# Rotary products and the probabilities' lower halves from GpSimd to VectorE in a two-layer attention and retention trunk

## The chip, the cores and the metric

The kernel runs on one core of a Trainium2 chip. Its engines are TensorE (PE in the profile; PEld is its loading of stationary operands), VectorE (DVE), ScalarE (ACT), GpSimd (POOL) and SyncE (SP), which here issues nearly all DMA transfers. The metric is the device time of one execution in microseconds. The time given for a kernel is the median of its runs; in addition one execution is recorded by the hardware profiler, and the profile comes from that one.

## What is computed

Two layers act on 2048 tokens of 1024 elements in float32. In each, the normed input is multiplied by a 1024 x 4096 matrix, whose columns are cut into the query, key, value and gate of eight attention heads of 64 and of four retention heads of 128.

```python
def hybrid_layer(x, norm_gain, w_in, w_out, rel_bias, cos, sin):
    hn = rms_norm(x, norm_gain)
    proj = hn @ w_in
    aq, ak, av, ag, rq, rk, rv, rg = jnp.split(proj, cuts, axis=-1)
    ya = chunked_rel_attention(aq, ak, av, rel_bias)      # 8 heads, own chunk of 64 + 8 before
    yr = chunkwise_retention(rq, rk, rv, cos, sin)        # 4 heads, rotary on rq and rk
    y = jnp.concatenate([ya * silu(ag), yr * silu(rg)], axis=-1)
    return x + y @ w_out

def apply_rotary(t, cos, sin):
    t1, t2 = jnp.split(t, 2, axis=-1)
    return jnp.concatenate([t1 * c - t2 * s, t1 * s + t2 * c], axis=-1)
```

The attention is a softmax over a band of nine chunks with a learned bias by distance. The retention multiplies masked, decayed products of rq and rk with rv, adds rq times a running state, and norms the result. A last rms_norm closes the trunk. The output is float32.

## The kernel before

**Split products.** [...] Every float32 operand is kept as an upper half (the value rounded to float16) and a lower half (what the rounding left), and a product is the sum of three: upper by upper, upper by lower, lower by upper. In the names, `whT`/`wlT` and `whV`/`wlV` are the two halves of the weights, `hTh`/`hTl` those of the normed tokens, transposed. An upper half is usually a copy by ACT; the lower half is a subtraction that follows.

**Loops.** Each of the two layers l has four sections s, each with two attention heads and one retention head. Within a section the tokens run in four blocks n of 512. For each (l, s, n) there are two dense passes. `dense_T` (L608 to 735) makes q, k, rq and rk (j = 0 to 3), each by 24 matmuls of 128 x 512: eight k-tiles times three split products. `dense_V` (L737 to 773) makes values and gates for four tiles a of 128 tokens (v, rv and the two gates, side by side in 512 columns), again 24 matmuls each. So each pass has 96 matmuls, cut by `yield` into 12 rounds of eight. In block (0, 0, 0), marked `first`, `dense_T` has a path of its own, since the weights and tokens are still arriving.

**What runs between the rounds.** `run` (L1117) steps a dense pass. After each round, `tick` fires the steps that were deferred with `later(k, fn)`: fn is issued k rounds later. Then comes one step of the attention generator of the block before, and then some steps of background work, given with `push(generator, steps)` and drawn by `pull` in proportion to the rounds left. The background work prepares the next weights (`prep_T`, `prep_V`, `prep_O`: load, squares, scale, two halves), norms tokens, and in section 2 takes the squares of the output weights (`prep_Omax`, L493: eight loads of 512 KB, a square by ACT for each, L309, and a sum by VectorE), from which the output weights' scale follows.

**Order.** PE, ACT, DVE and POOL run their instructions in program order, so what stands first on an engine's queue holds up what is behind it. SP's order is written out by hand up to the end of the first `dense_V`; after that the scheduler sets it.

**Rotary (L656 to 703).** ACT copies the raw product of rq or rk to `raw` (L662; for rq, `raw` is a view of the tile `rot`). `swap` has SP exchange its two halves of 64 partitions into `swp` with two transfers (L666, L667). Three rounds later (four for the first rq) `turn` issues three operations of 128 x 512 float32 on POOL: raw by the cosine table `tabc` (L670), swp by the sine table `tabs` (L671), and their sum (L672). Then ACT makes the upper half (L675), DVE the lower (L678), ACT a scaled copy for rq (L681), and for rk a transposing transfer makes `kt` (L685). `swp`, `tabc` and `tabs` have one buffer each, and `k`'s halves share the buffer of `swp`.

**Attention (L776 to 852).** There are eight units per block (four tiles of 128 queries by two heads), one in each three rounds. `qk` makes the scores S (L798, L799); DVE adds the bias and takes the maximum (L802, L804); ACT takes the exponential (L805) and copies the upper half into `pq` (L807); POOL subtracts to get the lower half (L808); one round later SP transposes both halves by a transfer into `pT` (L810). Two units later `pv` multiplies them with the values (L818 to 820), and DVE divides and gates (L824 to 830). A unit has 640 keys; in block 0 its four tiles have 128, 256, 384 and 512.

**Retention (L863 to 914).** One of four tiles in each two units. The first products (rk by rq) go in the first round of an even unit; then, by one round each, the mask by DVE (L872), the upper half by ACT (L857), the rest by DVE (L861, tile `dT`). The second products read `dT`, the values and the state's halves `sh` in the third round of the odd unit, five rounds after the first. POOL takes the power for the norm (L906). Both helpers for matmuls stand at L853.

**Bias.** At block 0 of a section, `bias_tiles` loads two bias tiles from a scratch in memory (`toep`), POOL fills two corners (L579, L580), and ACT scales (L581).

## Time and profile before

| | us |
|---|---|
| median of three runs | 2119.16 (2116.42 to 2122.45) |
| the profiled execution | 2117.65 |
| its span, first to last instruction | 2115.9 |
| TensorE busy in the span | 2010.4 |
| mean granted TensorE clock | 0.987 |

How to read the lines below. A row of the groups has line, engine, operation, output and input tile, shapes and count, then the busy time in all, the mean of one in ns, and the idle time of the engine just before these instructions with what ended it. A row of the waits has the engine and line that waited, what it waited for, then total, number and longest. A row of the timeline has start, duration and instruction, and in brackets how long the engine had been idle and what released it. SPq is SP's queue of issues. The profile has 40 equal slices of the span, 52.9 us each; a digit is a tenth of busy time, or of the clock that was granted to TensorE. "issue" is idle time without a recorded cause.

### The profile page before, as it was taken

What the parts mean: (1) busy time and instruction counts of PE and PEld (TensorE: products, weight loads), DVE (VectorE), ACT (ScalarE), POOL (GpSimd) and SP (SyncE); (2) the same over time, 40 slices, a digit from 0 to 9 for tenths busy, and PEclk for the clock granted to TensorE, in tenths of its full rate; (3) what the DMA queues carried; (4) which work ended last, traced back from release to release, by engine and by line L of the source; (5) the groups of instructions that cost most, each with busy time, mean ns of one, the idle gap of its engine ahead of it and who ended that gap; (6) DMA issues with size and microseconds to landing.
All of it is one profiled execution on the core that took longest, in us unless ns stands there. A gap on an engine that the chain in (4) does not pass through costs nothing.

```text
span 2115.9 us, 39456 instructions
## 1 busy us (share of the span) xinstructions
PE 2010.4 (95%) x14014; PEld 1052.1 (50%) x14014; DVE 1253.8 (59%) x3839; ACT 1139.1 (54%) x2522; POOL 679.5 (32%) x701
## 2 busy tenths in 40 slices
PE   6778999999999999988999999999999999999998
PEld 4334555555455555544444555555545555554543
DVE  7677566655565655566653556555656566556643
ACT  7455665556655654555444546554665465446432
POOL 1233333433343433321002343434333433433200
PEclk9899999999999999999999999999999999999999
DMA  8767675558665764699875556555685567548874
GB/s 247 165 119 164 137 164 113 115 110 191 148 113 111 159 158 99 132 197 259 206 187 115 121 103 140 123 124 103 149 186 119 101 137 169 123 101 182 217 193 127
DMA packets 645701, 313.63 MB, mean 148 GB/s; under 512 B 459232, under 2 KB 602080, under 8 KB 645504
## 3 DMA queue, kind: packets, MB, share of 16 engines
q1 hardware_dynamic: 645504, 311.12, 66.5%
q8 instruction: 109, 1.79, 0.4%
q14 instruction: 88, 0.72, 0.1%
HBM read 123.26 MB, written 41.98 MB: 78 GB/s over the span
## 4 chain that ended last, share of the span: by engine, by line
PE 47%; DMA 3%; ACT 2%; DVE 2%; issue 1%; POOL 1%; SPq 1%; POOLq 0%; DVEq 0%; ACTq 0%
PE dT L730 14%; PE dV L750 14%; PE dO L1090 12%; DMA pT<-pq 2%; PE r L853 2%; PE S L799 1%; PE S L798 1%; PE o L818 1%; PE o L819 1%; PE o L820 1%; DVE sc L802 1%; ACT sc L805 0%; ACT pq L807 0%; DMA yhy<-rhy 0%; DMA bias<-toep 0%
## 5 line engine op out<-in xcount | busy, mean ns | idle before, releaser
L808 POOL TENSOR_TENSOR pq<-sc,pq 128x640 f16<-128x640 f32 (+4 forms) x256 | 319.9, 1250 | 930.1 <-ACT pq L807 562.5
L805 ACT ACTIVATE sc<-sc,mq,cT 128x640 f32<-128x640 f32 (+4 forms) x256 | 218.5, 853 | 653.8 <-DVE rl L824 330.4
L730 PE MATMUL dT<-hTh,whT 128*128 128x512 f16 x1008 | 386.0, 383 | 11.9 <-DVE rv L766 7.8
L750 PE MATMUL dV<-wlV,hTh 128*128 128x512 f16 x1024 | 389.1, 380 | 6.9 <-DVE wlV L333 6.9
L750 PE MATMUL dV<-whV,hTh 128*128 128x512 f16 x1024 | 389.3, 380 | 6.2 <-DVE gt L768 6.1
L730 PE MATMUL dT<-hTl,whT 128*128 128x512 f16 x1008 | 386.2, 383 | 4.6 <-DMA hTl<-hTl 2.9
L750 PE MATMUL dV<-whV,hTl 128*128 128x512 f16 x1024 | 389.0, 380 | 0.0
L730 PE MATMUL dT<-hTh,wlT 128*128 128x512 f16 x1008 | 385.7, 383 | 0.0
L730 PEld LDWEIGHTS <-whT 128*128 128x128 f16 x2016 | 195.9, 99 | 236.7 <-issue 20.4
L750 PEld LDWEIGHTS <-hTh 128*128 128x128 f16 x2048 | 197.7, 98 | 223.9 <-DVE gt L768 9.1
L802 DVE CUSTOM_DVE_ANT_0 sc<-S,bias 128x640 f32<-128x640 f32 (+4 forms) x256 | 188.8, 737 | 154.7 <-PE S L799 150.8
L1090 PE MATMUL dO<-whO,yhy 128*128 128x512 f16 x512 | 194.8, 381 | 1.9 <-DMA yhy<-rhy 1.9
L1090 PE MATMUL dO<-whO,yly 128*128 128x512 f16 x512 | 194.6, 380 | 0.8 <-DMA yly<-rly 0.8
L1090 PE MATMUL dO<-wlO,yhy 128*128 128x512 f16 x512 | 194.6, 380 | 0.0
L807 ACT ACTIVATE pq<-sc 128x640 f16<-128x640 f32 (+4 forms) x256 | 171.5, 670 | 11.1 <-DMA pT<-pq 3.0
L1090 PEld LDWEIGHTS <-yhy 128*128 128x128 f16 x1024 | 99.9, 98 | 117.2 <-DMA yhy<-rhy 2.6
L750 PEld LDWEIGHTS <-hTl 128*128 128x128 f16 x1024 | 100.3, 98 | 115.8 <-issue 9.9
L730 PEld LDWEIGHTS <-wlT 128*128 128x128 f16 x1008 | 99.3, 98 | 106.4 <-issue 4.3
L818 PE MATMUL o<-v,pT 128*128 128x65 f16 x1120 | 129.8, 193 | 15.6 <-DMA pT<-pq 15.5
L798 PE MATMUL S<-k,q 128*128 128x128 f16 (+3 forms) x592 | 142.3, 267 | 0.7 <-DVE mq L802 0.7
L818 PEld LDWEIGHTS <-pT 128*128 128x128 f16 x1120 | 105.7, 97 | 51.0 <-DMA pT<-pq 21.5
L819 PE MATMUL o<-v,pT 128*128 128x64 f16 x1120 | 130.0, 195 | 0.0
(350 smaller groups left out, 3499.3 us busy)
## 6 DMA issues: line engine op xcount, KB each, us to landing
q<-qq SPq DMA_DIRECT2D x128, 128.0 KB, 2.5
yyy<-y_d SPq DMA_DIRECT2D x32, 512.0 KB, 4.6
stT<-in_w_in_dram SPq DMA_DIRECT2D x27, 512.0 KB, 4.8
stV<-in_w_in_dram SPq DMA_DIRECT2D x26, 512.0 KB, 4.4
k<-kk SPq DMA_DIRECT2D x128, 64.0 KB, 2.1
swp<-rot SPq DMA_DIRECT2D x64, 128.0 KB, 2.6
tabc<-tab SPq DMA_DIRECT2D x32, 256.0 KB, 2.7
tabs<-tab SPq DMA_DIRECT2D x32, 256.0 KB, 3.1
```

Source lines behind the costliest of these rows:

```text
L730: pe.matmul(ps, w_[:, j, kt, :], h_[:, kt, :], start=(m == 0), stop=(m == 23))
L750: pe.matmul(ps, h_[:, kt, a * P:(a + 1) * P], w_[:, kt, :], start=(m == 0), stop=(m == 23))
L798: pe.matmul(o, st.q[:, hx, 0, cs], k_, start=True, stop=False)
L799: pe.matmul(o, st.q[:, hx, 1, cs], k_, start=False, stop=True)
L802: dve.tensor_tensor_reduce(out=v, in0=S[:, 0:w], in1=g.bias[hx][:, 640 - w:640], scale=1.0, scalar=-3.0e38, op0=ALU.add, op1=ALU.max, accu ...
L805: act.activation(v, v, AF.Exp, bias=m[:, 0:1], scale=g.c[:, 0:1])
L807: act.activation(pq[:, 0:w], v, AF.Copy)
L808: pool.tensor_tensor(pq[:, w:2 * w], v, pq[:, 0:w], op=ALU.subtract)
L818: pe.matmul(o[:, 0:65], u.p[:, b, :], v_[:, 0:65], start=(b == 0), stop=False)
L819: pe.matmul(o[:, 0:64], u.p[:, b, :], v_[:, 65:129], start=False, stop=False)
L853: pe.matmul(out_, w_, m_, start=(i == 0), stop=(i + 1 == len(pairs)))
L1090: pe.matmul(ps, h_[:, kt, :], w_[:, kt, :], start=(m == 0), stop=(m == 23))
```

## The change

There are five edits.

1. The three rotary operations go from POOL to DVE and are issued one per round, in rounds d, d + 1 and d + 2 after the swap, instead of all three in round d. The upper half follows in d + 3, the lower in d + 4, the scaled copy in d + 5 (outside the first block it was d + 6). In the first block rq's d is 5 instead of 4, rk's swap is issued 8 rounds after its copy instead of 5, and its transposition 8 rounds after the swap instead of 7.
2. The lower half of the probabilities goes from POOL to DVE, one round after `qk` instead of in it, and the transposing transfer goes two rounds after `qk` instead of one.
3. `prep_Omax` is pushed in block 2 of section 2 instead of in block 0, again before the value pass.
4. In `dense_T`, tile j = 0 takes its 24 matmuls product by product: first whT by hTh for all eight k-tiles, then wlT by hTh, then whT by hTl. In `dense_V`, tile a = 0 takes all vh by hh, all vh by hl, then all vl by hh. The other tiles go k-tile by k-tile as before, with the three products in the new order.
5. In the retention of block (0, 0, 0) (`slow`) both kinds of products are issued in a unit's third round: the first products two rounds later than before, the second where they were.

```diff
-                    def turn():
-                        pool.tensor_tensor(raw, raw, st.tabc, op=ALU.mult)
-                        pool.tensor_tensor(swp, swp, st.tabs, op=ALU.mult)
-                        pool.tensor_tensor(raw, raw, swp, op=ALU.add)
+                    def turned(out_, x_, y_, op):
+                        return lambda: dve.tensor_tensor(out_, x_, y_, op=op)
...
-                    d = 4 if j == 2 and first else 3
-                    later(d, turn)
-                    later(d + 2 if first else d + 3, upper)
-                    later(d + 3 if first else d + 4, lower)
+                    d = 5 if j == 2 and first else 3
+                    later(d, turned(raw, raw, st.tabc, ALU.mult))
+                    later(d + 1, turned(swp, swp, st.tabs, ALU.mult))
+                    later(d + 2, turned(raw, raw, swp, ALU.add))
+                    later(d + 3, upper)
+                    later(d + 4, lower)
                     if j == 2:
-                        later(d + 4 if first else d + 6, third)
-                    if j == 3:
-                        later(7 if first else 11, tokens)
+                        later(d + 5, third)
+                    else:
+                        later(d + 5 if first else 11, tokens)
...
-                    later(5 if first else 2, swap)
+                    later(8 if first else 2, swap)
...
-            for kt in range(KT):
-                for (w_, h_) in ((g.h, hh), (g.h, hl), (g.l, hh)):
-                    pe.matmul(ps, w_[:, j, kt, :], h_[:, kt, :], start=(m == 0), stop=(m == 23))
+            terms = ((g.h, hh), (g.l, hh), (g.h, hl))
+            order = [(kt, w) for w in terms for kt in range(KT)] if j == 0 else [(kt, w) for kt in range(KT) for w in terms]
+            for kt, (w_, h_) in order:
+                pe.matmul(ps, w_[:, j, kt, :], h_[:, kt, :], start=(m == 0), stop=(m == 23))
...
-            for kt in range(KT):
-                for (w_, h_) in ((g.vh, hh), (g.vl, hh), (g.vh, hl)):
-                    pe.matmul(ps, h_[:, kt, a * P:(a + 1) * P], w_[:, kt, :], start=(m == 0), stop=(m == 23))
+            terms = ((g.vh, hh), (g.vh, hl), (g.vl, hh))
+            for kt, (w_, h_) in ([(kt, w) for w in terms for kt in range(KT)] if a == 0 else
+                                 [(kt, w) for kt in range(KT) for w in terms]):
+                pe.matmul(ps, h_[:, kt, a * P:(a + 1) * P], w_[:, kt, :], start=(m == 0), stop=(m == 23))
...
-            pool.tensor_tensor(pq[:, w:2 * w], v, pq[:, 0:w], op=ALU.subtract)
+            later(1, lambda: dve.tensor_tensor(pq[:, w:2 * w], v, pq[:, 0:w], op=ALU.subtract))
             u.p = b2.tile([P, 10, P], F16, tag="pT", name=f"pT{u.nm}")[:, 0:2 * nb, :]
-            later(1, lambda: sp.dma_start_transpose(out=u.p, in_=pq[:, 0:2 * w]))
+            later(2, lambda: sp.dma_start_transpose(out=u.p, in_=pq[:, 0:2 * w]))
...
+        slow = (l, s, n) == (0, 0, 0)
         for i, (a, hx) in enumerate(units):
             flow(1)
             u = qk(a, hx)
-            if i % 2 == 0:
+            if i % 2 == 0 and not slow:
                 next(ret, None)
             yield
             yield
-            if i % 2 == 1:
+            if i % 2 == 1 or slow:
                 next(ret, None)
...
-                if n == 0 and s == 2:
+                if n == 2 and s == 2:
                     push(prep_Omax(l, go), 13)
```

More of the change, by code (lines that the diff above doesn't have):

```diff
@@ L727, in dense_T @@
             m = 0
-            for kt in range(KT):
-                for (w_, h_) in ((g.h, hh), (g.h, hl), (g.l, hh)):
-                    pe.matmul(ps, w_[:, j, kt, :], h_[:, kt, :], start=(m == 0), stop=(m == 23))
-                    m += 1
-                    if m in (8, 16) or (m == 24 and first):
-                        yield
+            terms = ((g.h, hh), (g.l, hh), (g.h, hl))
+            order = [(kt, w) for w in terms for kt in range(KT)] if j == 0 else [(kt, w) for kt in range(KT) for w in terms]
+            for kt, (w_, h_) in order:
+                pe.matmul(ps, w_[:, j, kt, :], h_[:, kt, :], start=(m == 0), stop=(m == 23))
+                m += 1
+                if m in (8, 16) or (m == 24 and first):
+                    yield
             evacuate(j, ps)
@@ L747, in dense_V @@
             m = 0
-            for kt in range(KT):
-                for (w_, h_) in ((g.vh, hh), (g.vl, hh), (g.vh, hl)):
-                    pe.matmul(ps, h_[:, kt, a * P:(a + 1) * P], w_[:, kt, :], start=(m == 0), stop=(m == 23))
-                    m += 1
-                    if m in (8, 16):
-                        yield
+            terms = ((g.vh, hh), (g.vh, hl), (g.vl, hh))
+            for kt, (w_, h_) in ([(kt, w) for w in terms for kt in range(KT)] if a == 0 else
+                                 [(kt, w) for kt in range(KT) for w in terms]):
+                pe.matmul(ps, h_[:, kt, a * P:(a + 1) * P], w_[:, kt, :], start=(m == 0), stop=(m == 23))
+                m += 1
+                if m in (8, 16):
+                    yield
             rv = gp.tile([P, 3, P], F16, tag="rv", name=f"rv{nm}_{a}")
```

## The prediction

> **What bounds the kernel now.** I read the page first, then the waits of TensorE, the groups by shape, the windows of single stages, and the timeline wherever a wait named its place.
>
> ```profile
> span 2115.9 us, 39456 instructions
> PE 2010.4 (95%) x14014; PEld 1052.1 (50%) x14014; DVE 1253.8 (59%) x3839; ACT 1139.1 (54%) x2522; POOL 679.5 (32%) x701
> PE   6778999999999999988999999999999999999998
> PEclk9899999999999999999999999999999999999999
> ```
>
> TensorE is busy 95% of the span; its poorer slices are the first four (0 to 212 us) and the two where the layers meet. The change takes no matmul away, so all it can win lies in the 105.5 us in which TensorE is not busy and in the stretches at reduced clock. Who owns those 105.5 us is in TensorE's waits (total us, times, longest):
>
> ```profile
> PE r L853 <- DVE dT L861: 15.6, 10, 5.3
> PE o L818 <- DMA pT<-pq: 15.5, 11, 2.3
> PE r L853 <- ACT dT L857: 9.2, 3, 4.5
> PE dT L730 <- DVE rv L766: 7.8, 1, 7.8
> PE dV L750 <- DVE wlV L333: 6.9, 5, 1.6
> PE dV L750 <- DVE gt L768: 6.1, 5, 2.1
> PE dT L730 <- DMA hTl<-hTl: 2.9, 1, 2.9
> ```
>
> So the waits are few and long, not spread over 32 passes; each can be looked up. VectorE (59%) and GpSimd (32%) have room on average, but an average says nothing of a stage.
>
> **Moving work from GpSimd to VectorE.** The groups (line, engine, shapes, times | busy us, mean ns | idle before):
>
> ```profile
> L808 POOL TENSOR_TENSOR pq<-sc,pq 128x640 f16<-128x640 f32 x192 | 268.9, 1401 | 711.8 <-ACT pq L807 425.0 <-issue 243.0 <-DMA swp<-rot 36.0
> L671 POOL TENSOR_TENSOR swp<-swp,tabs 128x512 f32<-128x512 f32 x64 | 90.8, 1418 | 0.0
> L861 DVE SCALAR_TENSOR_TENSOR sh<-sh,state 128x128 f16<-128x128 f16 x120 | 87.4, 729 | 43.9 <-ACT sh L857 43.8
> L861 DVE SCALAR_TENSOR_TENSOR dT<-dT,r 128x128 f16<-128x128 f16 x128 | 35.4, 277 | 0.8 <-ACT dT L857 0.5
> L678 DVE TENSOR_TENSOR rot<-rot 128x512 f16<-128x512 f32 x32 | 34.4, 1074 | 37.0 <-ACT rot L675 37.0
> L678 DVE TENSOR_TENSOR rot<-raw,rot 128x512 f16<-128x512 f32 x32 | 21.8, 682 | 3.6 <-ACT rot L675 3.6
> L231 DVE TENSOR_TENSOR rln<-xnn,rhn 128x1024 f16<-128x1024 f32 x6 | 7.3, 1224 | 8.1 <-ACT rhn L227 8.1
> ```
>
> Prices on VectorE: the two L678 rows are a two-operand operation of 512 elements with f32 input; the undisturbed one is 0.68 us, and I take 0.69 for each of the 192 rotary products: 132 us. For the 640-element subtraction I go between 0.68 (512) and 1.22 (1024): 0.68 + 128 × (1.22 − 0.68)/512 = 0.82 us; 192 of these are 157 us, and the 64 smaller ones (512 down to 128) about 31. Bounds: it can't be below the 512 row (0.68) nor above GpSimd's 1.40. Added: some 320 us. What comes back: the same instruction on the same shape takes 0.277 us as dT and 0.729 as sh, and L678 0.682 or 1.074; the slow ones stand where GpSimd works. (729 − 277) × 120 is 54 us and (1074 − 682) × 32 is 13; other lines have smaller losses of this kind, so I take 110 in all (bounds 0 and 130). VectorE would stand near 1254 + 320 − 110 = 1460 us, 69%. The Trainium skill ("Advanced Engine Details and Errata", VectorE Performance Modes, Mode Summary) says that GpSimd shares VectorE's second memory port and that the two block each other; the rows above agree with it. By it nearly all of that stretch vanishes, as GpSimd keeps only 258 of its 706 instructions; if the slow rows had another cause, nothing would come back, and the time would be rival A's, 2136.
>
> VectorE isn't on the path on average; it is where a pass is short of room. Four value halves of section 2 in layer 0 (blocks 1, 2, 3, then block 0 of section 3); columns: us, then busy time of PE, PEld, DVE, ACT, POOL, then clock, DMA share, GB/s:
>
> ```profile
> 561.40:586.00 24.60, 24.60 (x165) 12.54 (x162) 16.60 (x61) 15.18 (x41) 11.43 (x12) 1.00 0.50 116
> 611.90:637.90 26.00, 26.00 (x207) 14.34 (x204) 15.51 (x47) 13.79 (x36) 14.16 (x14) 1.00 0.44 94
> 664.00:690.10 26.10, 26.10 (x209) 14.43 (x207) 16.91 (x55) 17.18 (x41) 13.78 (x14) 1.00 0.51 111
> 716.90:744.30 27.40, 26.06 (x205) 14.23 (x203) 18.26 (x54) 16.63 (x39) 14.55 (x16) 1.00 0.75 158
> ```
>
> A half is 12 rounds (26.0/12 = 2.17 us each) and four attention units (6.5 us each). It gets four subtractions (3.3) and all six products (4.1), and returns (54 + 13)/32 = 2.1 us of stretch by the two rows alone. Block 3: 16.91 + 7.4 − 2.1 = 22.2 of 26.1, 85%; block 1: 21.9 of 24.6, 89%; block 2: 20.8 of 26.0, 80%. With nothing returned block 3 would stand at 93%, block 1 at 98%. It fits, but VectorE runs in program order, and it has one thing that is due:
>
> ```profile
> 686.59 0.28 DVE L861 SCALAR_TENSOR_TENSOR dT<-dT,r 128x128 f16<-128x128 f16 x1
> 681.02 1.28 DVE L333 SCALAR_TENSOR_TENSOR wlV<-stV,sV,whV 128x1024 f16<-128x1024 f32 x1
> L853 PE MATMUL r<-rv,dT x7: 219/219/219, 663.8 to 689.9; 128*128 128x128 f16 x7
> ```
>
> The rest of the masked products ends here at 686.87, and the matmul that reads it is the last of the third row, at 689.9: 3.0 us of slack, one and a half rounds. In the fullest unit (the one with the weight preparation's 1.28) VectorE works about 7 of 6.5 us after the change, and stands about 1 us more while ACT makes the upper half that the subtraction needs. The lag is 1.5 to 2 us, under 3.0. I charge 3 us in all for units in which it runs over (0 to 15).
>
> The transposition of the probabilities goes one round later, though the subtraction itself is 0.6 us shorter and its input no later. TensorE's wait for it is 15.5 us in 11 places already; I charge +3 (−4 to +10). The rotary products wait for the swapped copy, now on VectorE's queue instead of GpSimd's. At block 0 that copy is late:
>
> ```profile
> 508.42 1.27 POOL L670 TENSOR_TENSOR rot<-rot,tabc 128x512 f32<-128x512 f32 x1 [0.47 <-DMA swp<-rot]
> POOL rot L670 <- DMA swp<-rot: 12.9, 8, 9.3
> ```
>
> The second product reads what landed just then; behind it on VectorE would stand the next unit's maximum (L802), for which ACT's exponential and, two units on, TensorE wait. The second row counts GpSimd's waits for it: eight, one of 9.3 at the start, the others short. I charge six places with 0 to 2 us each: +4 (0 to 12). The Trainium skill ("Perfetto Trace Analysis", Tensor Engine Instruction) calls VectorE's execution queue strictly first in, first out; it speaks against the change at this place, and no row read here shows VectorE passing a waiting instruction. Were it not so, this term would be 0 and the time 2097.
>
> **The start.** Here the products' place matters most:
>
> ```profile
> 58.94 2.02 POOL L670 TENSOR_TENSOR rot<-rot,tabc 128x512 f32<-128x512 f32 x1 [4.37 <-DMA tabc<-tab]
> 64.56 0.63 ACT L675 ACTIVATE rot<-rot 128x512 f16<-128x512 f32 x1 [4.85 <-POOL rot L672]
> 64.55 0.48 SPq L666 DMA_DIRECT2D swp<-raw  x1
> 66.09 1.30 SPq L236 DMA_TRANSPOSE hTh<-hTh  x1
> 72.92 1.30 SPq L236 DMA_TRANSPOSE hTh<-hTl  x1
> 76.35 0.58 PE L730 MATMUL dT<-hTh,whT 128*128 128x512 f16 x1 [7.78 <-DVE rv L766]
> 79.87 0.59 PE L730 MATMUL dT<-hTl,whT 128*128 128x512 f16 x1 [2.94 <-DMA hTl<-hTl]
> 68.00:86.00 18.00, 7.28 (x25) 2.85 (x24) 10.82 (x27) 4.07 (x9) 4.92 (x8) 0.62 1.01 230
> ```
>
> GpSimd's three products take 5.6 us from the table's landing. Until 64.55 SP stands at the second swap (its buffer is free only after L672), and behind it on SP are the transpositions of the next tokens, issued one by one from 66.09 on; TensorE's 7.78 (put down to VectorE, long done; it is the transposed tokens) and 2.94 wait for the last of them, and the last column but two says the clock fell to 0.62. After the change the built programs' order has the transpositions of two token tiles ahead of that swap, the swap of rk leaves at round 8 instead of 5, and three products of 0.69 end nearer 62. The products save 3.5 us, the two swap issues 1 more, so I estimate 4.5 us off the first wait; most of the second (2.5) follows the same issues; and 2 us less are lost at the low clock: −9. Bounds: −14 (both waits and the clock's loss gone) to −5 (the two swap issues alone).
>
> In block (0,0,0)'s retention the first products move two rounds later and the second stay: three rounds between them instead of five, for a chain of mask, ACT, VectorE. The longest waits there are already for that:
>
> ```profile
> 123.20 0.29 PE L853 MATMUL r<-rv,dT 128*128 128x128 f16 x1 [5.30 <-DVE dT L861]
> 535.67 0.39 PE L853 MATMUL r<-rv,dT 128*128 128x128 f16 x2 [3.89 <-ACT dT L857]
> 1561.78 0.39 PE L853 MATMUL r<-rv,dT 128*128 128x128 f16 x2 [4.50 <-ACT dT L857]
> 534.63 0.83 ACT L581 ACTIVATE bias<-bias,ciT 128x640 f32<-128x640 f32 x1 [1.48 <-POOL bias L580]
> 504.30:536.40 32.10, 26.79 (x206) 14.42 (x204) 16.89 (x58) 22.88 (x51) 14.47 (x15) 0.99 1.01 233
> ```
>
> But the first products' input comes two rounds later too, so it no longer waits for rotary: +2 (−4 to +8). The 5.30 and its like near the start have work in front that GpSimd stretches: −2 (−8 to +4).
>
> **The output weights.** The second and third rows of the last fence are the dearest waits outside the start. Their chain: in section 2, block 0, eight loads of the output weights run beside that section's bias loads and the weights' own (DMA share 1.01, against 0.44 in block 2); the bias lands late, ACT stands at L581 till 534.63, the products' upper half (L857) is behind it on ACT, TensorE behind that. Moved to block 2, where DMA has 56% and ACT 47% to spare, both waits go (−8.4), and with them what I estimate at 5 us of low clock behind them (bounds 0 and 6). New cost at block 2: squares and loads in a half where ACT was busy 13.8 of 26; +1.4 (0 to 8). Sum −12.
>
> **The matmul order.** With the lower-weight product last in tile 0, the first use of wlV moves 15 matmuls back: 15/8 of a round, 4 us, against waits of at most 1.6. The 6.9 us of five waits go; I add half a us for what they pull along: −7.5 (−3 to −8). The waits for gt (6.1) are for a buffer, not for weights, and stay. The end of layer 0 is 0 ± 3.
>
> **Sum:** −9 + 2 − 2 + 3 + 4 + 3 − 12 − 7.5 + 0 = −18.5. The profiled run took 2117.65 us, 1.75 more than its span and 1.5 below the median of 2119.16: 2117.65 − 18.5 + 1.5 = 2100.7, say 2101.
>
> **The rivals.**
> (A) VectorE becomes the bound in the 16 value halves of blocks 1 and 3, where weights are prepared. For it: 85 to 89%, and one queue in order. Against it: 3.0 us of slack against 2 of lag. It decides once the lag passes 3.0 us; two tokens in each half late by 1.2 us each are 16 × 2 × 1.2 = 38 us, on top of the forecast without its own 3: 2101 − 3 + 38 = 2136. With the stretch returned it is the less likely; with none (93 to 98%) it would be the likeliest.
> (B) The start gains nothing, since the short gap of the first retention eats what the transpositions win: 2101 + 9 = 2110.
> (C) The waits only move: the output weights stall block 2 as they did block 0 (+12), and the five weight waits come back as waits for buffers behind a fuller VectorE (+4): 2117, no change.
>
> **How the numbers follow.** Forecast 0.55, A 0.20, B 0.12, C 0.13. The terms' bounds, added as squares (5, 6, 6, 7, 6, 8, 6, 3, 3 and half of 12), give ±17 around the forecast: its own range is 2084 to 2118. To hold eight of ten it reaches towards A, and to the terms' better ends below: 2078 to 2128. 0.3%, 6.4 us, is about what a measurement here can tell from no change. Faster by more: nearly all of the forecast, most of B, a third of C: 0.66; slower: nearly all of A and a little of the rest: 0.20; between: 0.14.
>
> **What would show it.** In the changed profile: the 5.6 us at L670 to L672 gone and TensorE's waits of 7.78 and 2.94 down to about 3.6 together; no wait of TensorE for ACT's dT near 535 and 1561, none for wlV; L861's sh near 0.28 us, the subtraction near 0.82 and VectorE near 69%. It is wrong if waits of r L853 for DVE dT L861 appear in every value half of blocks 1 and 3 (A), if those for the transposed probabilities grow past 30 us, or if block 2 of section 2 shows new waits (C).

## The result, and the profile after

| | before | changed |
|---|---|---|
| median of 20 runs each, us | 2116.49 (2112.13 to 2122.45) | 2121.18 (2118.20 to 2127.45) |
| ratio, 95% interval | | 1.0025 [1.0017, 1.0032] |
| profiled execution, us | 2117.65 | 2122.58 |
| its span, us | 2115.9 | 2120.4 |

The changed kernel is slower by a quarter of a per cent: little, but the whole interval, from 20 runs each, lies above 1. A gain was forecast (2101, 15 us under the 2116.5 of these runs). The time lies within the forecast's range of 2078 to 2128.

The head of the page of the changed kernel (busy time, share of the span, count):

```profile
span 2120.4 us, 39355 instructions
PE 2014.7 (95%) x14014; PEld 1050.2 (50%) x14014; DVE 1415.8 (67%) x4287; ACT 1139.6 (54%) x2522; POOL 110.7 (5%) x253
```

The time in which TensorE isn't busy is the same 106 us (2120.4 − 2014.7; 2115.9 − 2010.4 before), so waits won and waits lost cancel. The 4.5 us between the spans stand in its busy time, 4.3 us more than before. The granted clock is not the reason, with a mean of 0.989 against 0.987; what stretched the busy time is not shown. VectorE went to 67%; 69% was forecast. The groups on VectorE (line, shapes, times | busy us, mean ns | idle before):

```profile
L810 DVE TENSOR_TENSOR pq<-sc,pq 128x640 f16<-128x640 f32 x192 | 157.9, 823 | 126.6 <-ACT pq L809 126.5 <-ACT raw L662 0.2
L670 DVE TENSOR_TENSOR rot<-rot,tabc 128x512 f32<-128x512 f32 x32 | 22.1, 691 | 48.7 <-DMA swp<-rot 41.0 <-DMA y_d<-yr 6.8 <-DMA tabc<-tab 1.0
L864 DVE SCALAR_TENSOR_TENSOR sh<-sh,state 128x128 f16<-128x128 f16 x120 | 34.0, 283 | 0.0
L676 DVE TENSOR_TENSOR rot<-rot 128x512 f16<-128x512 f32 x32 | 21.9, 683 | 0.7 <-ACT rot L673 0.7
```

The prices were right: 0.82 us for the subtraction, 0.69 for a product, and sh and the lower half of rq fell from 0.73 and 1.07 to 0.28 and 0.68 us, now that GpSimd is nearly idle. The last column has the waits: VectorE stands 126.6 us in front of the subtraction, waiting for ACT's upper half (0.66 us each; the prediction had about 1 in a full unit), and 48.7 us in front of rq's first product, 41.0 of them for the swapped copy. The experiments below ask what these waits hold up behind them.

TensorE's waits (total us, times, longest):

```profile
PE o L820 <- DMA pT<-pq: 22.1, 18, 3.2
PE r L856 <- DVE dT L864: 13.7, 15, 4.0
PE dT L731 <- DMA hTh<-hTl: 9.6, 1, 9.6
PE r L856 <- ACT dT L860: 6.7, 9, 2.8
PE S L800 <- DVE mq L804: 5.7, 2, 3.0
PE dV L752 <- DVE gt L770: 5.2, 6, 1.6
```

The last but one of these was short before:

```profile
PE S L798 <- DVE mq L802: 0.7, 2, 0.4
```

The waits for wlV are gone, and those for the start's lower tokens (2.9 us before). The first token wait went from 7.8 to 9.6, that for transposed probabilities from 15.5 to 22.1 and that for VectorE's maxima (`mq`) from 0.7 to 5.7. The sign of rival A, waits for VectorE's `dT` in every value half of blocks 1 and 3, did not come: of their 13.7 us 8.8 lie in the first section, and no value half of a block 1 or 3 outside it has more than 0.4.

Where the time is won and lost shows best in when each pass begins. The table has the first matmul of a pass by the timelines, as a difference to the kernel before; "base" and "all mended" are two of the experiments below (e4 and e15). A column that stays the same from row to row says that the passes between took as long as in the kernel before. The profiled execution of the base was the slowest of its four (2099.5 us, median 2094.2).

| pass (layer, section, block) | before, us | changed | base | all mended |
|---|---|---|---|---|
| T 0,0,1 | 76.3 | +2.8 | −0.1 | +0.3 |
| V 0,0,1 | 105.0 | +5.2 | −3.8 | −2.5 |
| T 0,1,0 | 268.7 | −1.4 | −5.3 | −9.7 |
| T 0,2,0 | 477.1 | +2.0 | −6.1 | −7.1 |
| V 0,2,1 | 561.4 | −5.8 | −13.6 | −14.6 |
| V 0,2,3 | 664.0 | +1.9 | −9.5 | −11.3 |
| V 0,3,3 | 870.6 | +0.9 | −10.5 | −12.0 |
| first output product, layer 0 | 900.9 | +5.0 | −10.5 | −12.4 |
| T 1,0,0 | 1099.6 | +1.2 | −11.3 | −18.3 |
| V 1,2,1 | 1588.1 | −6.4 | −18.4 | −28.9 |
| V 1,2,3 | 1690.7 | +3.1 | −16.0 | −25.2 |
| V 1,3,3 | 1899.1 | +1.3 | −18.0 | −23.2 |
| first output product, layer 1 | 1929.5 | +5.0 | −18.0 | −23.6 |

In the changed kernel, the squares' move wins 7.8 us (layer 0) and 9.1 us (layer 1) by block 1 of section 2, and 7.7 and 9.5 us are lost again in blocks 2 and 3; the start wins nothing; and the last block of each layer loses 4 us.

**The start.** Timeline of the changed kernel, VectorE, SP's issues, TensorE:

```profile
64.00 0.69 DVE L670 TENSOR_TENSOR rot<-rot,swp 128x512 f32<-128x512 f32 x1
72.20 0.50 SPq L666 DMA_DIRECT2D swp<-raw  x1
73.44 1.56 SPq L236 DMA_TRANSPOSE hTh<-hTl  x1
75.10 2.66 SPq L237 DMA_TRANSPOSE hTl<-hTl  x1
79.14 1.44 PE L731 MATMUL dT<-hTh,whT 128*128 128x512 f16 x3 [9.64 <-DMA hTh<-hTl]
```

The products end at 64.69, against 64.52 before: each is short, but they go one per round with the tokens' halves between. The last pair of transpositions is issued at 73.44 and 75.10, behind the second swap, against 72.92 and 74.94, and TensorE starts at 79.14 instead of 76.35. Only 0.5 of these 2.8 us is the later issue; the rest is that TensorE starts 5.7 us after the issue instead of 3.4. Which of the transfers around it slows that transposition is not shown.

**VectorE's queue in section 2, block 2**, changed kernel:

```profile
608.69 0.69 DVE L670 TENSOR_TENSOR rot<-rot,tabc 128x512 f32<-128x512 f32 x1 [3.56 <-DMA swp<-rot]
625.40 0.16 DVE L506 TENSOR_TENSOR omaxO<-omaxO,m1O0m 128x1 f32<-128x1 f32 x1 [2.79 <-ACT stO0m L309]
626.67 0.81 DVE L810 TENSOR_TENSOR pq<-sc,pq 128x640 f16<-128x640 f32 x1
```

How long VectorE stood at these sums in layer 0 (us, times; layer 1 has the same):

```profile
  ACT stO0m L309: 9.1, 5
```

A sum of 0.16 us holds the queue for 2.79, since ACT makes its square after the unit's exponential and upper half. Only then come the unit's division and the subtraction; with the subtraction on GpSimd, the latter would not have stood there. Windows of the value halves that the prediction weighed (us, busy PE, PEld, DVE, ACT, POOL, clock, DMA share, GB/s):

```profile
555.70:581.50 25.80, 24.87 (x164) 12.37 (x161) 19.91 (x67) 15.67 (x40) 1.09 (x2) 1.00 0.47 110
607.70:637.70 30.00, 26.93 (x207) 14.14 (x205) 19.36 (x64) 19.99 (x47) 1.09 (x2) 1.00 0.82 194
665.90:692.00 26.10, 26.10 (x209) 14.42 (x207) 20.70 (x65) 16.97 (x41) 1.10 (x2) 1.00 0.52 114
718.50:745.20 26.70, 26.03 (x204) 14.11 (x201) 22.18 (x65) 16.55 (x39) 1.39 (x4) 1.00 0.81 165
```

In block 3 VectorE is busy 20.70 of 26.10 us (79%) and TensorE all of it. Block 2, with less on VectorE (19.36), takes 30.0 us instead of 26.0. So VectorE's load doesn't order the halves.

**The layer's end**, first the kernel before, then the changed one:

```profile
882.14 1.23 SPq L236 DMA_TRANSPOSE yhy<-rhy  x1
885.34 0.82 DVE L802 CUSTOM_DVE_ANT_0 sc<-S,bias 128x640 f32<-128x640 f32 x1 [1.69 <-DMA yhy<-rhy]
```

```profile
884.84 1.72 SPq L236 DMA_TRANSPOSE yhy<-rhy  x1
889.30 0.82 DVE L804 CUSTOM_DVE_ANT_0 sc<-S,bias 128x640 f32<-128x640 f32 x1 [4.54 <-DMA yhy<-rhy]
890.18 0.22 PE L800 MATMUL S<-k,q 128*128 128x128 f16 x1 [2.79 <-DVE mq L804]
```

The scores' tile shares its buffers with the rows for the output product, whose transposition is issued 2.7 us later. VectorE waits 4.54 us for it, against 1.69 before, and TensorE 2.79 us for VectorE's maximum.

### The profile page after: what moved, and what is told of

Read it like the earlier page. It is cut to its first block, busy times and chain, and to the rows that moved or that the text cites. A ratio compares the mean times of both kernels' runs of the same rounds, so it can differ in the third digit from the quotient of the medians.

```text
span 2120.4 us, 39355 instructions
## 1 busy us (share of the span) xinstructions
PE 2014.7 (95%) x14014; PEld 1050.2 (50%) x14014; DVE 1415.8 (67%) x4287; ACT 1139.6 (54%) x2522; POOL 110.7 (5%) x253
## 4 chain that ended last, share of the span: by engine, by line
PE 62%; DVE 14%; ACT 10%; DMA 9%; issue 3%; SPq 2%; POOL 0%; POOLq 0%; DVEq 0%; ACTq 0%
PE dT L731 20%; PE dV L752 17%; PE dO L1093 14%; DMA pT<-pq 4%; ACT sc L807 3%; PE r L856 2%; DVE sc L804 2%; PE S L800 2%; PE S L801 2%; DVE pq L810 1%; ACT pq L809 1%; PE o L820 1%; PE o L821 1%; PE o L822 1%; DMA swp<-rot 1%
## 5 line engine op out<-in xcount | busy, mean ns | idle before, releaser
L731 PE MATMUL dT<-hTh,whT 128*128 128x512 f16 x1008 | 349.6, 383 | 12.6 <-DMA hTh<-hTl 9.6
L752 PE MATMUL dV<-whV,hTh 128*128 128x512 f16 x1024 | 354.9, 383 | 5.2 <-DVE gt L770 5.2
L752 PE MATMUL dV<-wlV,hTh 128*128 128x512 f16 x1024 | 353.6, 381 | 0.0
L752 PE MATMUL dV<-whV,hTl 128*128 128x512 f16 x1024 | 353.6, 381 | 0.0
L731 PE MATMUL dT<-hTh,wlT 128*128 128x512 f16 x1008 | 348.1, 381 | 0.0
L731 PE MATMUL dT<-hTl,whT 128*128 128x512 f16 x1008 | 346.8, 379 | 0.0
L810 DVE TENSOR_TENSOR pq<-sc,pq 128x640 f16<-128x640 f32 (+4 forms) x256 | 189.3, 739 | 149.3 <-ACT pq L809 146.9
L809 ACT ACTIVATE pq<-sc 128x640 f16<-128x640 f32 (+4 forms) x256 | 171.5, 670 | 10.5 <-DMA pT<-pq 2.5
L820 PE MATMUL o<-v,pT 128*128 128x65 f16 x1120 | 130.2, 194 | 24.1 <-DMA pT<-pq 22.1
L909 POOL TENSOR_TENSOR rss<-rss,mhalf 128x1 f32<-128x1 f32 x128 | 73.2, 572 | 1444.5 <-DVE rss L908 1429.6
L820 PEld LDWEIGHTS <-pT 128*128 128x128 f16 x1120 | 105.5, 97 | 64.6 <-DMA pT<-pq 37.1
```

Of the source, the lines that this page charges most:

```text
L731: pe.matmul(ps, w_[:, j, kt, :], h_[:, kt, :], start=(m == 0), stop=(m == 23))
L752: pe.matmul(ps, h_[:, kt, a * P:(a + 1) * P], w_[:, kt, :], start=(m == 0), stop=(m == 23))
L809: act.activation(pq[:, 0:w], v, AF.Copy)
L810: later(1, lambda: dve.tensor_tensor(pq[:, w:2 * w], v, pq[:, 0:w], op=ALU.subtract))
L820: pe.matmul(o[:, 0:65], u.p[:, b, :], v_[:, 0:65], start=(b == 0), stop=False)
L909: pool.tensor_tensor(ss, ss, mhalf, op=ALU.pow)
```

## The experiments

Times are medians of four to ten executions; the kernel before had 2116.8, 2116.3, 2116.7 and 2115.3 us beside the four groups of runs, so numbers of different groups can be set side by side. The intervals of the ratios are about ±0.1% to ±0.2% (2 to 4 us). The passes' starts tell places, but they come from one execution each.

**e1: the sums of squares later (in the changed kernel).** The part not shown regroups the rounds left free behind the sums, from four to five.

```diff
-            if j == 0:
-                dve.tensor_copy(mm, m1)
-            else:
-                dve.tensor_tensor(mm, mm, m1, op=ALU.add)
+            later(2, lambda j=j, m1=m1, mm=mm: dve.tensor_copy(mm, m1) if j == 0 else dve.tensor_tensor(mm, mm, m1, op=ALU.add))
...
```

> The changed kernel, but each sum of the output weights' squares is issued two rounds after its square instead of right behind it. Theory Q (one queue: VectorE stands up to 2.8 us at these sums, with the probabilities' subtraction behind them): the passes of section 2, blocks 2 and 3, lose less than half of the 6.3 us (layer 0) and 7.9 us (layer 1) that they lose against the kernel before; median some 8 us under the changed kernel, near 2113. Rival X (the extra transfers and ACT's squares are what hurts there): the losses stay above 5 us each and the time within 2 us of the changed kernel.

2112.6 us, ratio 0.9979 [0.9969, 0.9989]: 8.6 under the changed kernel, near the 2113 that theory Q had, and VectorE no longer stands for ACT's squares at the sums. Its profiled execution was the slowest of its ten (2120.0), and in it layer 0 still lost 6.0 us over blocks 2 and 3 and layer 1 3.7, against 7.7 and 9.5, so the expected halving missed in layer 0: the sums are a part, not all of the loss there.

**e2: the subtraction back on GpSimd (in the changed kernel).**

```diff
-            later(1, lambda: dve.tensor_tensor(pq[:, w:2 * w], v, pq[:, 0:w], op=ALU.subtract))
+            pool.tensor_tensor(pq[:, w:2 * w], v, pq[:, 0:w], op=ALU.subtract)
...
-            later(2, lambda: sp.dma_start_transpose(out=u.p, in_=pq[:, 0:2 * w]))
+            later(1, lambda: sp.dma_start_transpose(out=u.p, in_=pq[:, 0:2 * w]))
```

> The changed kernel with the lower half of the probabilities back on GpSimd, transposed one round after qk. Theory Q: the losses at section 2, blocks 2 and 3, fall to under 2 us a layer, VectorE's later lag goes too, and the median is 10 to 16 us under the changed kernel, 2105 to 2111. Rival X: the losses there stay, and the time is within 3 us of the changed kernel.

2119.6 us, ratio 1.0007 [0.9995, 1.0019]: 1.5 under the changed kernel. The expectation missed: blocks 2 and 3 still lose 3.4 and 6.1 us, though the subtraction no longer stands behind the sums. In this run sh takes 0.763 us in the mean again, beside GpSimd's subtractions.

**e3: the rotary products back on GpSimd (in the changed kernel).** Its rounds are those of the kernel before; `slow` stays.

```diff
-                    later(d, turned(raw, raw, st.tabc, ALU.mult))
-                    later(d + 1, turned(swp, swp, st.tabs, ALU.mult))
-                    later(d + 2, turned(raw, raw, swp, ALU.add))
+                    later(d, turn)
...
-                    later(8 if first else 2, swap)
+                    later(5 if first else 2, swap)
```

> The changed kernel with the rotary products back on GpSimd at the rounds of the kernel before, the first block's swap too. If late swapped copies that stop VectorE are the dear part, section 1's first passes (+3.5 us) and the passes into the output products (+4 us a layer) give most of that back, 8 us in all; if they are not, less than 3 us come back beside the start. At the start either way: the first token wait as in the changed kernel or worse.

2109.0 us, ratio 0.9962 [0.9949, 0.9975]: 12.2 come back, more than expected. At the start the expectation missed: the first token wait fell to 6.9 us.

**e4, the base: matmul order and squares' place alone (in the kernel before).** In both dense passes the order is the change's.

```diff
+            terms = ((g.h, hh), (g.l, hh), (g.h, hl))
+            order = [(kt, w) for w in terms for kt in range(KT)] if j == 0 else [(kt, w) for kt in range(KT) for w in terms]
...
-                if n == 0 and s == 2:
+                if n == 2 and s == 2:
```

> The kernel before with only the new matmul order and the output weights' squares at block 2. If both edits bring what the prediction says (7.5 and 12 us) where VectorE is not loaded further, the median is 18 to 22 us under the kernel before, 2095 to 2099. If the squares stall block 2 by themselves (X), it is 8 us under it at most, 2108 or more.

2094.2 us, ratio 0.9897 [0.9876, 0.9919]: 22.6 under the kernel before. What the prediction hoped of these two edits was there; the other three eat all of it, and 27 us altogether.

**e5: base with the subtraction on VectorE.**

```diff
-            pool.tensor_tensor(pq[:, w:2 * w], v, pq[:, 0:w], op=ALU.subtract)
+            later(1, lambda: dve.tensor_tensor(pq[:, w:2 * w], v, pq[:, 0:w], op=ALU.subtract))
...
-            later(1, lambda: sp.dma_start_transpose(out=u.p, in_=pq[:, 0:2 * w]))
+            later(2, lambda: sp.dma_start_transpose(out=u.p, in_=pq[:, 0:2 * w]))
```

> The base here is the run with only the matmul order and the squares moved (2094.2 us); to it only the subtraction on VectorE is added, with its later transposition. Theory Q (VectorE stands for ACT's copy in front of the subtraction, and what follows is late): 4 to 10 us over the base, lost in passes whose block prepares weights or squares (section 2, blocks 2 and 3) and in the first blocks, nothing elsewhere. If the subtraction is free in itself and the first block's new retention was what cost 15 us in the run with GpSimd's rotary products, it stays within 3 us of the base.

2104.2 us, ratio 0.9942 [0.9927, 0.9957]: 10.0 over the base, the upper end of what was expected. The places were not: by the passes' starts, 4.0 us are lost in section 1 of layer 0, where nothing was expected, beside 3.6 and 4.5 in section 2's blocks 2 and 3.

**e6: base with rotary on VectorE outside the first block.**

```diff
+                    if first:
+                        d = 4 if j == 2 else 3
+                        later(d, turn)
...
+                    d = 3
+                    later(d, turned(raw, raw, st.tabc, ALU.mult))
+                    later(d + 1, turned(swp, swp, st.tabs, ALU.mult))
+                    later(d + 2, turned(raw, raw, swp, ALU.add))
+                    later(d + 3, upper)
+                    later(d + 4, lower)
```

> The base (2094.2 us) with the rotary products on VectorE, one per round from the third round on, except in the first block, which stays as it was. Theory Q (late swapped copies stop VectorE, 41 us of waits in the changed kernel): 6 to 12 us over the base, with VectorE's waits for swp above 40 us. If the start of the program is what made rotary on VectorE dear, it stays within 3 us of the base.

2114.0 us, ratio 0.9987 [0.9977, 0.9996]: 19.8 over the base, more than expected. Who waited for the tile swp (us, times):

```profile
  DVE rot L675: 59.5, 26
```

**e7: the same, rq's products two rounds later.**

```diff
-                    d = 3
+                    d = 5 if j == 2 and n < 3 else 3
...
-                        later(11, tokens)
+                        later(9 if n < 3 else 11, tokens)
...
-                    later(5 if first else 2, swap)
+                    later(5 if first else (4 if n < 3 else 2), swap)
```

> As the run before it, but rq's products are issued from the fifth round after the swap on (blocks 0 to 2), rk's swap two rounds later. Theory Q: VectorE's waits for swp fall under 15 us, and at least half of what the run before it loses against the base comes back. Rival V (VectorE has too little room in the value passes): the time stays within 2 us of the run before it.

2108.5 us, ratio 0.9958 [0.9943, 0.9974]: 5.4 of the 19.8 come back, and the waits did not fall as expected:

```profile
  DVE rot L675: 37.6, 20
  DVE raw L675: 11.1, 13
```

My reading, which e11 tests: the two rounds put no instruction that waits for TensorE between, and VectorE comes to the product as soon as it has done the unit's maximum, whatever round it was issued in.

**e8: base with the sums later.** The edit of e1 in the base.

```diff
+            later(2, lambda j=j, m1=m1, mm=mm: dve.tensor_copy(mm, m1) if j == 0 else dve.tensor_tensor(mm, mm, m1, op=ALU.add))
```

> The base (2094.2 us) with the sums of the output weights' squares two rounds later. Theory Q: GpSimd makes the subtraction here, so VectorE's stop at a sum delays less; of the 4.1 and 2.4 us that the base loses in section 2, blocks 2 and 3, some 2 to 4 us come back, 2090 to 2092. Rival X: nothing comes back.

2090.9 us, ratio 0.9877 [0.9862, 0.9892], as expected. It beats both kernels. In layer 0 VectorE's stops at the sums fell from 11.1 us (7) in the base to 1.9 (1).

**e9: base with the change's first block alone**, its rotary on VectorE, its swap at round 8, `slow`.

```diff
+                    if not first:
+                        later(3, turn)
...
+                    d = 5 if j == 2 else 3
+                    later(d, turned(raw, raw, st.tabc, ALU.mult))
...
+                    later(8 if first else 2, swap)
...
+        slow = (l, s, n) == (0, 0, 0)
```

> The base (2094.2 us) with the change's first block alone: there the rotary products on VectorE, rk's swap at round 8, and the first retention's later products. The prediction had 7 us of gain in it (9 less 2). Theory S (the token transpositions are bound by SP's issuing one by one, and the short gap of the retention costs): 3 to 9 us over the base, all of it before the first pass of section 1.

2101.5 us, ratio 0.9932 [0.9916, 0.9947]: 7.3 over the base, where the prediction had 7 under. Two of its waits of TensorE:

```profile
PE dT L745 <- DMA hTh<-hTl: 9.4, 1, 9.4
PE r L870 <- ACT dT L874: 12.6, 5, 5.7
```

The wait for the tokens is as long as in the changed kernel, and that for ACT's dT, 3.7 us in the base, is 12.6, while that for VectorE's dT falls from 16.6 to 13.3: a net 5.6 us, where the prediction had +2 for the gap of three rounds and −2 for VectorE's dT. By the passes' starts 4.7 us are lost before section 1.

**e10: base with the subtraction on VectorE, transposed in the same round.**

```diff
-            pool.tensor_tensor(pq[:, w:2 * w], v, pq[:, 0:w], op=ALU.subtract)
+            later(1, lambda: dve.tensor_tensor(pq[:, w:2 * w], v, pq[:, 0:w], op=ALU.subtract))
...
             later(1, lambda: sp.dma_start_transpose(out=u.p, in_=pq[:, 0:2 * w]))
```

> The base with the subtraction on VectorE, as in the run that was 10 us over it, but with the transposition issued in the same round as the subtraction (one round after qk, as before). If the later round of the transposition is what costs, most of the 10 us come back (2095 to 2099). Theory Q (the subtraction itself stands on VectorE's queue behind other work and holds what follows): 2101 or more.

2102.5 us, ratio 0.9940 [0.9917, 0.9963]: the transposition's round is worth 1.7 of the 10 us, less than the intervals can tell, and the subtraction itself the rest.

**e11: base with rotary on VectorE, rq's products a unit later.** Against e6:

```diff
-                    d = 3
+                    d = 6 if j == 2 and n < 3 else 3
...
-                        later(11, tokens)
+                        later(9 if n < 3 else 11, tokens)
...
-                    later(5 if first else 2, swap)
+                    later(5 if first else (5 if n < 3 else 2), swap)
```

> The base with rotary on VectorE, rq's products from the sixth round after the swap on (blocks 0 to 2), so behind the next attention unit's maximum, which the fifth round was not. Theory Q: VectorE's waits for swp fall to under 15 us now, outside blocks 3, and the time is 2096 to 2104, under that of the fifth round (2108.5). Rival V: 2108 or more.

2104.3 us, ratio 0.9949 [0.9931, 0.9967], 0.3 over the expected range: half of the 19.8 is back.

```profile
  DVE rot L675: 17.5, 8
```

One round further than e7, but behind the next maximum: now the copy has landed. Of the waits that are left, 9.9 us are for the products of block 3, which kept the early place, and 6.6 stand at the start of layer 1.

**e12: the matmul order alone (in the kernel before).** As e4, with the squares where they were:

```diff
-                if n == 2 and s == 2:
+                if n == 0 and s == 2:
```

> The kernel before with the new matmul order alone. The prediction has 7.5 us for it; the passes' starts of the base up to section 2 say 6, with three waits for wlV behind that, some 9 in all: 2105 to 2110. The rest of the base's 22 us, 12 to 16, is then the moved squares'.

2102.8 us, ratio 0.9942 [0.9924, 0.9959]: 13.9 under the kernel before, more than expected. Beside wlV's 6.9 us, TensorE's waits have no row any more for the lower halves of the tokens (the 2.9 that the prediction quotes, and this one of the kernel before), since the new order uses hTl last in tile 0:

```profile
PE dT L730 <- DMA hTl<-rln: 1.6, 2, 0.9
```

These 11.4 us are TensorE's whole gain in idle time (105.5 before, 94.2 here). Its busy time is 5.2 us shorter (2005.2), with a mean granted clock of 0.991 instead of 0.987.

**e13: e8 with the subtraction on VectorE, transposed in its round.** The edits of e8 and e10:

```diff
+            later(2, lambda j=j, m1=m1, mm=mm: dve.tensor_copy(mm, m1) if j == 0 else dve.tensor_tensor(mm, mm, m1, op=ALU.add))
...
+            later(1, lambda: dve.tensor_tensor(pq[:, w:2 * w], v, pq[:, 0:w], op=ALU.subtract))
```

> The base with the later sums (2090.9 us), and to it the subtraction on VectorE with its transposition in the same round (8.3 us over the base without the later sums). Theory Q with the place named: the subtraction costs where it stands behind the sums of squares, so now it costs 0 to 4 us, 2091 to 2095, and section 2's blocks 2 and 3 lose under 2 us a layer. Theory G (a general cost of one more instruction per unit on VectorE's queue): 7 us or more, 2098 or above.

2096.9 us, ratio 0.9907 [0.9888, 0.9925]: 6.0 over e8, between the two theories. By the passes' starts, set against e8's, blocks 2 and 3 of layer 0's section 2 cost nothing now (+6.8 before them, +6.3 after); what is lost is lost in sections 0 and 1 (+5.8 by their end). The groups show what remains on both engines, and sh:

```profile
L809 DVE TENSOR_TENSOR pq<-sc,pq 128x640 f16<-128x640 f32 x192 | 170.6, 889 | 150.6 <-ACT pq L808 150.5
L670 POOL TENSOR_TENSOR swp<-swp,tabs 128x512 f32<-128x512 f32 x64 | 92.5, 1445 | 0.0
L862 DVE SCALAR_TENSOR_TENSOR sh<-sh,state 128x128 f16<-128x128 f16 x120 | 33.8, 282 | 0.5 <-ACT sh L858 0.5
```

The subtraction takes 0.889 us instead of 0.823, beside a GpSimd that still has the rotary products; sh takes 0.28 us already, with the subtraction alone moved. That the longer subtraction costs the 6 us is not shown: TensorE idles 87.8 us here and 87.2 in e8, and the difference lies in its busy time (2007.8 against 2001.7).

**e14: e11 with block 3 on GpSimd.**

```diff
+                    if n == 3:
+                        later(3, turn)
+                        later(6, upper)
+                        later(7, lower)
+                        later(9 if j == 2 else 11, third if j == 2 else tokens)
+                        return
```

> As the run with rq's products a unit later (2104.3 us), but block 3 of each section keeps its rotary products on GpSimd. If what is left of rotary's cost sits at the layers' ends, where the last block's products delay the rows for the output product, the 4 us that each layer loses before its first output product vanish: 2095 to 2098. Rival V (VectorE's load in all value passes): 2101 or more.

2102.1 us, ratio 0.9937 [0.9918, 0.9956]: not the time expected, and by the time alone on rival V's side. The place was right: the 4 us before the first output product (3.9 in each layer in e11, against the base's 0.0) are gone in both layers. With GpSimd making the subtractions, the stretch is worse than in the kernel before:

```profile
L884 DVE SCALAR_TENSOR_TENSOR sh<-sh,state 128x128 f16<-128x128 f16 x120 | 101.4, 845 | 38.1 <-ACT sh L880 37.5
```

Whether this makes the 7.9 us over the base is not shown: the profiled executions of the two, 2100.4 and 2099.5 us, hardly differ.

**e15: all mended**: both on VectorE, the sums later, transposition in its round, rq's products a unit later; block 3 and the first block as before. The edits of e13 and e14:

```diff
+                    d = 6 if j == 2 else 3
+                    later(d, turned(raw, raw, st.tabc, ALU.mult))
...
+            later(1, lambda: dve.tensor_tensor(pq[:, w:2 * w], v, pq[:, 0:w], op=ALU.subtract))
```

> All together: the sums later, the subtraction on VectorE and transposed in its round, rotary on VectorE a unit later in blocks 0 to 2, on GpSimd in block 3 and the first block. If the move to VectorE costs only by what it stands behind: 2091 to 2098, no gain over the base with later sums. If the moves cost by load: 2103 or more. A gain over 2090.9 would say that GpSimd's neighbourhood costs something after all.

2091.2 us, ratio 0.9884 [0.9861, 0.9907]: the same as e8, the base with later sums, though VectorE is busy 66% of the span instead of 60%:

```profile
PE 2003.7 (96%) x14014; PEld 1048.1 (50%) x14014; DVE 1391.0 (66%) x4233; ACT 1139.8 (54%) x2522; POOL 186.8 (9%) x307
L883 DVE SCALAR_TENSOR_TENSOR sh<-sh,state 128x128 f16<-128x128 f16 x120 | 33.9, 283 | 0.0
```

So both moves together cost nothing in the median once the sums, the transposition and the products stand in better places, and win nothing either. Each alone was slower: e13 by 6.0 us than e8, e14 by 7.9 than the base. Why is open. e14 lacks the later sums, and e15 met a better granted clock: 0.994 in the mean of its four executions, against 0.992 in e8 and 0.9895 in e14.

## Why the prediction was wrong

Four runs are nested, and their medians make the ledger: 2116.7 before, 2102.8 with the order (−13.9), 2094.2 with the squares moved (−8.6), 2101.5 with the first block's part (+7.3), 2121.2 with everything (+19.7). The prediction had −7.5, −12, −7 and +10, with −2 for other waits near the start.

Part of these steps is TensorE's granted clock. I estimate what the lower clock took as (1 − mean granted clock) × span, averaged over a kernel's executions; it is an upper estimate, as TensorE idles in some of that time. It is some 25 us before, 21.5 with the order, 16.8 in the base, 22.0 with the first block's part and 23.4 with everything; so −3, −5, +5 and +1 of the four steps may be the clock. In e15 it is 12.5, against 16.2 in e8.

- **The matmul order** was right in kind and undersized. Its waits for wlV went as said. The step overlooked that tile 0 of `dense_T` now uses the lower tokens last too, so their 4.5 us of waits go as well (2.5 of them had been counted under the start). Together these are 11.4 us; the rest is of the size of the clock's 3.
- **The output weights' squares** were right in kind: alone, 8.6 us against 12. The two long waits for ACT's dT went, as the changed kernel's −5.8 and −6.4 at block 1 show, and so did the low clock at them: 0.89 and 0.83 from 530 to 545 and from 1555 to 1575 us in the kernel before, 1.00 in the base where its passes have these places (517 to 532 and 1537 to 1555). The base has other such stretches, one of 0.72 from 625 to 631. "New cost at block 2", priced at 1.4 (0 to 8), is the term that failed in the changed kernel: blocks 2 and 3 lose 7.7 us in layer 0 and 9.5 in layer 1 (4.1 and 2.4 in the base). I priced ACT's and the transfers' room and not the eight sums on VectorE in each layer, five of which stand for ACT, 9.1 us in all, with the subtraction behind them. e1 gives 8.6 back for moving the sums. With the subtraction on GpSimd the same move gives some 3 (e8).
- **The start** failed at one sentence: "the products save 3.5 us". They are shorter, but are issued one per round and end at the same time. SP issues the transpositions one by one, which the quoted rows showed, and the moved swap comes in front of the last pair. The short gap of the first retention, priced at +2 with −2 for other waits near the start, costs a net 5.6 us in e9. So what had been worked out as −9 + 2 − 2 measured +7.3, some 5 of which may be the clock.
- **The late swap**, priced at +4 for "six places with 0 to 2 us each", was counted too low: VectorE stands for the copy in 26 of the 31 later blocks in e6, 59.5 us. The trace before told of it: in the row of L808 that I quoted, this copy ended 36.0 us of GpSimd's idle time, and I read past it. The move of the rotary products alone costs 19.8 us there, and e11, one unit later, gives 9.7 of them back. At the layer's end the products of block 3 cost 4 us in each layer, which the prediction had at 0 ± 3: e14 has them back on GpSimd and the 4 us are gone.
- **VectorE's load.** Rival A was given 0.20 and has fallen: the halves of blocks 1 and 3 run at 77 and 79% of VectorE (89 and 85 were worked out), block 3 with TensorE busy all through. e15 has 75% in block 1 at no cost; its block 3, with rotary on GpSimd, has 68%. The prices came out as worked out. The stretch that returned was undersized: 1253.8 + 320 − 1415.8 = 158 us instead of 110, above the bound of 130, which is why VectorE stands at 67% and not at 69%. The Trainium skill ("SBUF — State Buffer", Who interferes with whom) has it that an instruction of VectorE with two inputs in SBUF contends with one of GpSimd that reads SBUF; the rows of sh agree (0.73 us before, 0.28 after). I used the rule as a gain of the change only. The stretch of sh goes with GpSimd's subtraction: 0.28 us in e3, e5, e10 and e13, which move the subtraction and not rotary, 0.76 to 0.85 in e2, e6 and e14, where rotary moved and the subtraction stayed.
- **The rivals.** Nearest was (C), that the waits only move: it named the place (block 2) and gave 2117. Its second half, waits for buffers, did not come (gt 5.2 us, 6.1 before), and the start and the late swaps, which it lacked, make the rest. (B), that the start gains nothing, was right in kind and too mild.
- **Small slips.** The page has 701 instructions of GpSimd, of which 253 stayed, not 706 and 258; and the squares of the bounds add to ±18, not ±17. Neither changes the forecast.

Not tried: `slow` by itself in the first block, since the later rotary there needs it. Nor was e14 with the later sums, so the price of rotary alone in its best place is open. How the 19.7 us of the last step divide isn't settled: alone the subtraction costs 10.0 and rotary 19.8, together less.

## What to carry to other kernels

Before moving work to an engine that runs in order, list what it will stand for there and what stands behind it. The room that the engine has on average decided little here: with better places, and block 3 and the first block left on GpSimd, the same moves took 2091 us instead of 2121. Moving an instruction by rounds helped little (e7) until it passed one that waits for TensorE, the engine that sets the pace (e11). Try two moves that relieve the same engine together as well as one by one: here each alone cost 6 to 8 us and both together nothing, for a reason that is not shown. And e8, as fast as any kernel here, moves no work from one engine to another.

## What was not expected of the hardware

The row of sh tells which of GpSimd's instructions stretch it: 0.73 us before, 0.85 with most of rotary moved to VectorE (e14), 0.28 with the subtraction alone moved (e13) and with both (e15). So it may be a reason for e14's time, but not for e13's. And SP needs 1.25 to 3.1 us to issue one transposition of 128 x 1024 in the start, so eight in a row are a chain of their own.
